# Roots by GpSimd's power and weight remainders by an accumulating DMA, in a two-layer diffusion trunk

## The chip, the cores and the metric

The kernel runs on one core of one Trainium2 chip. The metric is the device time of one execution in microseconds. Three timed runs of the kernel before took 2482.03, 2484.36 and 2476.64 us, so the median is 2482.03 us.

The engines are called PE (TensorE; PEld is its weight load), DVE (VectorE), ACT (ScalarE), POOL (GpSimd) and SP (SyncE, which here issues every DMA).

## The reference, cut to what matters

Two token streams of width 1024 (512 latent tokens and 128 context tokens) pass through two layers with the same weights. All arithmetic is float32.

```python
def rmsnorm(x, g):
    xf = x.astype(jnp.float32)
    y = xf * lax.rsqrt(jnp.mean(xf * xf, axis=-1, keepdims=True) + EPS)
    return (y * g.astype(jnp.float32)).astype(x.dtype)

def merge_branches(out_a, out_b, out_c, gates, lp, lam_init):
    oa = rmsnorm(out_a.reshape(B, L, A_HEADS, A_V), lp['a_subln_g']) * (1.0 - lam_init)
    ya = oa.reshape(B, L, A_WIDTH) @ lp['w_br_a']
    ...
    ga, gb, gc = jnp.split(jax.nn.sigmoid(gates), N_BRANCH, axis=-1)
    return (ga * ya + gb * yb + gc * yc) @ lp['w_out']

def latent_mixers(h, lp, lam, lam_init, cache, cos, sin):
    qa, ka, va, qb, kb, vb, qc, kc, vc, gates = project_heads(h, lp['w_in'])
    qb = apply_rope(rmsnorm(qb, lp['b_qnorm_g']), cos, sin)
    kb = apply_rope(rmsnorm(kb, lp['b_knorm_g']), cos, sin)
    ...

def trunk_layer(x, cvec, lp, mix_fn):
    sh1, sc1, g1, sh2, sc2, g2 = modulation(cvec, lp['w_mod'], lp['b_mod'])
    mixed, kv = mix_fn(rmsnorm(x, lp['norm1_g']) * (1.0 + sc1) + sh1)
    x = x + g1 * mixed
    x = x + g2 * swiglu(rmsnorm(x, lp['norm2_g']) * (1.0 + sc2) + sh2, lp['w_ffn_in'], lp['w_ffn_out'])
```

The norms that the change touches are those of `qb` (8 heads of 64), of `kb` (2 heads of 64) and of branch A's output (4 heads of 128). Each needs a reciprocal square root of a few numbers per token.

## The kernel before, in words

Each float32 product runs as three products in the faster type fp32r. A weight chunk of 128x1024 is loaded into `raw`. ACT copies it to `whi` (rounded to fp32r), POOL computes the remainder `wlo = raw - whi`, and PE multiplies `whi` with the high and low halves of the data and `wlo` with the high half (lines 410 to 412 for products with 320 columns, 718 to 720 for those with 256). There are 268 chunks. The buffers hold two `raw`, four `whi` and four `wlo`; `raw` is given back to the loader when `wlo` is done.

In each layer the first 60 chunks carry the q, k, v projections, the gates and the branch projections. They are used while the three attentions run, in the order of `STEPS`: the PE works on "dense" products wherever an attention item isn't ready. After them come the output projection (chunks from `O_WO` on), the second norm and the two parts of the FFN.

The order of every engine's instructions is fixed when the program is built. `_Order.run` is a list scheduler: tasks are Python generators that yield an engine, an estimated cost and a priority, and the scheduler picks the earliest by its estimates (`dve` is 0.068 us + 0.00104 us per element, `ptt` on POOL is 0.147 + 0.0021 per element). On the chip each engine runs its own list in that order and waits on semaphores, so an engine that stands at one instruction holds back all that is behind it.

The names that the change touches are these. `weights` has three tasks: `load` (SP's DMA into `raw`), `hi` (ACT's copy into `whi`) and `lo` (POOL's remainder into `wlo`). `rsqrt` computes 1/sqrt of a 128xn tile, with n of 2 (k norm), 4 (q norm) or 5 (branch A), on DVE alone: two integer instructions make a first guess in `rs_y`, and three Newton steps of three instructions each follow, with `rs_u` as scratch. `qk_norm` calls it 15 times in a layer and `a_head` four times, 38 calls in all. `rope` and `qk_norm` also use POOL for sums and products that feed the transposes of q and k (tiles `nat` and `st`).

Of the kernel before, what the change touches and what calls it, by code (L numbers as in the profile page):

```python
# [23 lines left out]

F32 = mybir.dt.float32
F32R = mybir.dt.float32r
I32 = mybir.dt.int32
AF = mybir.ActivationFunctionType
ALU = mybir.AluOpType
AX = mybir.AxisListType  # L30
# [2 lines left out]
P = 128  # L33
# [12 lines left out]
EPS = 1e-6  # L46
THETA = 10000.0
CH = 1024
MAGIC = 0x5F3759DF

C_ID, C_C, C_FG, C_END = 0, 128, 144, 152
S_N1, S_N2, S_BM, S_SUB, S_END = 0, 8, 16, 64, 65
# [6 lines left out]
O_WO = O_BR + 3 * N_BR  # L59
# [21 lines left out]


MOD_SOON, MOD_SPREAD = 0.7, 1.4
ENGINES = ("PE", "ACT", "DVE", "POOL", "SP")


# [4 lines left out]
class _Event:  # L91
    def __init__(self):
        self.t = None
        self.tasks = []
# [11 lines left out]
class _Order:  # L106


    def __init__(self):
        self.free = {e: 1.5 if e == "SP" else 2.9 for e in ENGINES}  # L110
        self.pend = {e: [] for e in ENGINES}
        self.slots = {}
# [75 lines left out]
    def run(self):  # L188
        while True:
            best = None  # L190
            for e in ENGINES:
                lst = self.pend[e]
# [31 lines left out]
def _n(ap):  # L224
    n = 1
    for d in ap.shape[1:]:
        n *= d
    return n
# [27 lines left out]
class _Trunk:  # L256
# [95 lines left out]
    def dma(self, out, in_, bytes_):  # L352
        return ("SP", max(0.45, bytes_ / 3.5e5), lambda: self.nc.sync.dma_start(out=out, in_=in_), 2.2)

    def weights(self, plan):

        self.chunks = []
        todo = []  # L360
        for p in plan:
            c = {"src": p, "loaded": self.ev(), "hi_ok": self.ev(), "lo_ok": self.ev()}
            todo.append(c)
        self.chunks = list(todo)

        def load(c):
            c["raw"] = yield from self.get("raw", [P, CH])
            yield self.dma(c["raw"], self.I["w"][c["src"]], 128 * 4 * CH)
            self.o.fire(c["loaded"])

        def hi():
            for c in todo:
                yield self.wait(c["loaded"])
                yield ("acq", "whi")
                yield ("acq", "wlo")
                c["hi"], c["lo"] = self.t("whi", [P, CH], F32R), self.t("wlo", [P, CH], F32R)
                yield self.act(c["hi"], c["raw"], AF.Copy)
                self.o.fire(c["hi_ok"])

        def lo():  # L380
            for c in todo:
                yield self.wait(c["hi_ok"])
                yield self.ptt(c["lo"], c["raw"], c["hi"].bitcast(F32), ALU.subtract)
                self.rel("raw")
                self.o.fire(c["lo_ok"])

        def load_rest():
            yield self.wait(todo[1]["loaded"])
            for c in todo[2:]:
                yield from load(c)  # L390

        for g in (load_rest, hi, lo):
            self.o.spawn(g(), 20)
        return [lambda c=c: load(c) for c in todo[:2]]
# [22 lines left out]

    def rsqrt(self, v, shape):

        nc = self.nc  # L420
        y = yield from self.get("rs_y", shape)
        u = yield from self.get("rs_u", shape)
        n = _n(v)
        yield self.dve(n, lambda: nc.vector.tensor_scalar(
            u.bitcast(I32), v.bitcast(I32), 1, None, op0=ALU.logical_shift_right))
        yield self.dve(n, lambda: nc.vector.tensor_scalar(
            y.bitcast(I32), u.bitcast(I32), -1, MAGIC, op0=ALU.mult, op1=ALU.add))
        for _ in range(3):
            yield self.tt(u, y, y, ALU.mult)
            yield self.stt(u, u, -0.5, v, ALU.mult, ALU.mult)  # L430
            yield self.stt(y, u, 1.5, y, ALU.add, ALU.mult)
        self.rel("rs_u")
        return y

# [261 lines left out]
    def qkv_unit(self, evac, n_slots, events):  # L696
# [51 lines left out]
        def run_by_rows():  # L748
# [13 lines left out]
            for b in (NB - 1, *range(NB - 1)):  # L762
                self.o.spawn(after(b, *ds[b]), 30 + 0.1 * b - (NB - 1 - b == 0))

        return run, run_by_rows

    def rope(self, x, b, groups, k=None):
# [788 lines left out]
    def layer(self, l, h, norm1, close):  # L1556
# [53 lines left out]
        def dense():  # L1610
            steps = _steps()
            if l == 0:
                yield from unit(*steps.pop(0))[1]()
            else:
                two = [unit(*steps.pop(0))[0] for _ in range(2)]
                for blocks in (range(2), range(2, NB)):
                    for run in two:
                        yield from run(blocks)
            for kind, i in steps:
                yield from step(kind, i)  # L1620
            yield self.wait(x2_open)
            halves = [(m, e) for m in range(WO_SPLIT) for e in range(2)]
            halves += [(m, e) for e in range(2) for m in range(WO_SPLIT, KT)]
            yield from self.out_proj(l, halves, x2, ssq2, ssq2_ok)
            o.fire(out_done)
            yield self.wait(f_open)
            for part in PARTS:
                yield from self.ffn_in(part, h2[0], h2[1], act, act_ok)
                if part[-1] == NF - 1:
                    yield self.wait(ssq3_open)  # L1630
                yield from self.ffn_out(l, part, act, act_ok, x2, ssq3, ssq3_ok, not last)
            o.fire(ffn_done)
# [144 lines left out]
    def run(self):  # L1777
        nc, I = self.nc, self.I
# [11 lines left out]
        pool, _ = self.bufs["c"]  # L1790
        one = lambda tag, shape: pool.tile(shape, F32, tag=tag, name=tag, bufs=1)
        con = one("con", [P, C_END])
        self.ident = con[:, C_ID:C_ID + P]
        self.fg = con[:, C_FG:C_FG + 8]
        self.ones, self.eps = one("ones", [P, P]), one("eps", [P, 1])
        cact = one("cact", [P, 16])
        self.cact = cact.rearrange("p (k c) -> p k c", k=KT)
        self.small, self.modc, self.acol, self.g1h, self.mod_ok = [], [], [], [], []
# [6 lines left out]
        nc.sync.dma_start(out=con, in_=I["con"])  # L1805
        nc.vector.memset(self.ones, 1.0)
        nc.vector.memset(self.eps, EPS)
        nc.scalar.activation(cact, con[:, C_C:C_C + 16], AF.Silu)
        for l in range(DEPTH):
            nc.sync.dma_start(out=self.small[l], in_=I["sm"][l])  # L1810
# [180 lines left out]
```

## Time and profile before

| | |
|---|---|
| median of three runs | 2482.03 us (2476.64 to 2484.36) |
| the profiled execution | 2480.7 us |
| its span, first to last instruction | 2478.9 us |
| mean granted TensorE clock | 0.983 of full speed |
| busy: PE, DVE, ACT, POOL | 96%, 66%, 44%, 37% |
| attention stages (PE interleaves attention and dense work) | about 62 to 640 us and 1302 to 1860 us of the span |

The profile comes from one execution on the chip. A line such as "L338 DVE ... x57 | 20.9, 373 | 0.4" tells source line, engine, output and input tiles, the count, busy microseconds and the mean nanoseconds of one, and then the idle time of the engine just ahead of these instructions with what ended it. The attention and FFN stages have different limits, so shares over the whole span say little about either.

### The profile page before, as it was taken

What the parts mean: (1) busy time and instruction counts of PE and PEld (TensorE: products, weight loads), DVE (VectorE), ACT (ScalarE), POOL (GpSimd) and SP (SyncE); (2) the same over time, 40 slices, a digit from 0 to 9 for tenths busy, and PEclk for the clock granted to TensorE, in tenths of its full rate; (3) what the DMA queues carried; (4) which work ended last, traced back from release to release, by engine and by line L of the source; (5) the groups of instructions that cost most, each with busy time, mean ns of one, the idle gap of its engine ahead of it and who ended that gap; (6) DMA issues with size and microseconds to landing.
All of it is one profiled execution on the core that took longest, in us unless ns stands there. A gap on an engine that the chain in (4) does not pass through costs nothing.

```text
span 2478.9 us, 44317 instructions
## 1 busy us (share of the span) xinstructions
PE 2381.0 (96%) x17084; PEld 2332.7 (94%) x17084; DVE 1646.1 (66%) x3924; ACT 1097.4 (44%) x2566; POOL 907.2 (37%) x656
## 2 busy tenths in 40 slices
PE   7998889999999999999989998999999999999997
PEld 4998889999988999999989997999999999999997
DVE  7588898678799666676677879887774462212224
ACT  5666566556323322122257664666552342212221
POOL 3534322433433433333345434224333343333331
PEclk9999999999999999999999999999999999999999
DMA  6211111111454444344422111101112322222221
GB/s 235 88 45 57 38 43 35 48 52 44 145 191 141 153 143 150 133 156 139 150 88 70 53 59 43 35 29 63 44 52 73 106 77 77 77 77 71 75 77 60
DMA packets 84739, 216.54 MB, mean 87 GB/s; under 512 B 9648, under 2 KB 23600, under 8 KB 84272
## 3 DMA queue, kind: packets, MB, share of 16 engines
q1 hardware_dynamic: 84528, 213.71, 25.6%
q8 instruction: 135, 2.21, 0.4%
q14 instruction: 76, 0.62, 0.1%
HBM read 206.85 MB, written 6.82 MB: 86 GB/s over the span
## 4 chain that ended last, share of the span: by engine, by line
PE 76%; DVE 18%; issue 2%; ACT 1%; DMA 1%; POOL 0%; SPq 0%; DVEq 0%; ACTq 0%
PE S L411 12%; PE S L410 12%; PE S L412 12%; PE B L410 6%; PE B L412 6%; PE B L411 6%; PE B L1024 3%; PE B L718 3%; PE B L720 3%; PE B L719 3%; PE S L996 2%; PE S L995 2%; DVE nu L338 2%; DVE P L346 2%; PE B L1260 2%
## 5 line engine op out<-in xcount | busy, mean ns | idle before, releaser
L350 POOL TENSOR_TENSOR wlo<-raw,whi 128x1024 fp32r<-128x1024 f32 x268 | 659.6, 2465 | 906.6 <-ACT whi L311 906.2
L411 PE MATMUL S<-h,whi 128*128 128x320 f32 x1408 | 438.7, 312 | 6.5 <-DVE h L338 5.8
L410 PE MATMUL S<-h,whi 128*128 128x320 f32 x1408 | 438.5, 311 | 0.0
L412 PE MATMUL S<-h,wlo 128*128 128x320 f32 x1408 | 437.4, 311 | 0.0
L311 ACT ACTIVATE whi<-raw 128x1024 fp32r<-128x1024 f32 x268 | 282.8, 1056 | 271.7 <-PE S L411 227.2
L718 PE MATMUL B<-whi,h 128*128 128x256 f32 x928 | 278.3, 300 | 1.0 <-DVE u L334 0.5
L411 PEld LDWEIGHTS S<-h,whi 128*128 128x128 f32 x1408 | 266.1, 189 | 9.4 <-DVE h L338 7.0
L720 PE MATMUL B<-whi,h 128*128 128x256 f32 x928 | 266.3, 287 | 3.7 <-DVE h L338 3.1
L410 PEld LDWEIGHTS S<-h,whi 128*128 128x128 f32 x1408 | 266.1, 189 | 0.8 <-ACT h L311 0.4
L412 PEld LDWEIGHTS S<-h,wlo 128*128 128x128 f32 x1408 | 266.3, 189 | 0.0
L719 PE MATMUL B<-wlo,h 128*128 128x256 f32 x928 | 265.7, 286 | 0.0
L515 DVE SCALAR_TENSOR_TENSOR md<-mr,cb 128x512 f32<-128x512 f32 x320 | 260.2, 813 | 5.5 <-DMA mr<-wt 0.8
L410 PE MATMUL B<-h,whi 128*128 128x320 f32 x768 | 245.2, 319 | 1.0 <-ACT th L311 1.0
L412 PE MATMUL B<-h,wlo 128*128 128x320 f32 x768 | 238.5, 311 | 0.0
L411 PE MATMUL B<-h,whi 128*128 128x320 f32 x768 | 238.2, 310 | 0.0
L334 DVE TENSOR_TENSOR s<-s,S 128x320 f32<-128x320 f32 x88 | 42.9, 488 | 281.2 <-ACT s L311 281.2
L311 ACT ACTIVATE P<-S,mx 128x768 f32<-128x768 f32 (+4 forms) x240 | 180.6, 754 | 88.3 <-DVE mx L1009 68.8
L410 PE MATMUL S<-act,whi 128*128 128x320 f32 x704 | 218.2, 310 | 0.0
L411 PE MATMUL S<-act,whi 128*128 128x320 f32 x704 | 217.8, 309 | 0.0
L412 PE MATMUL S<-act,wlo 128*128 128x320 f32 x704 | 217.7, 309 | 0.0
L410 PE MATMUL B<-u,whi 128*128 128x320 f32 x640 | 203.3, 318 | 5.2 <-ACT u L311 4.0
L411 PE MATMUL B<-u,whi 128*128 128x320 f32 x640 | 199.4, 312 | 0.8 <-DVE u L334 0.7
(162 smaller groups left out, 5918.3 us busy)
## 6 DMA issues: line engine op xcount, KB each, us to landing
raw<-w SPq DMA_DIRECT2D x268, 512.0 KB, 3.3
mr<-wt SPq DMA_DIRECT2D x160, 256.0 KB, 3.0
mraw<-wm SPq DMA_DIRECT2D x24, 256.0 KB, 4.8
x<-x SPq DMA_DIRECT2D x8, 320.0 KB, 5.6
xr<-x SPq DMA_DIRECT2D x16, 160.0 KB, 3.2
xm<-x SPq DMA_DIRECT2D x8, 320.0 KB, 4.3
xr<-xm SPq DMA_DIRECT2D x16, 160.0 KB, 2.6
y<-h SPq DMA_DIRECT2D x16, 160.0 KB, 1.8
```

Source lines behind the costliest of these rows:

```text
L311: fn = lambda: self.nc.scalar.activation(out, in_, func, **kw)
L338: _n(out), lambda: self.nc.vector.scalar_tensor_tensor(out, a, s, b, op0=op0, op1=op1),
L346: _n(out), lambda: self.nc.vector.tensor_scalar(out, a, s1, s2, op0=op0, **kw), not _in_psum(a), cols
L350: return ("POOL", 0.147 + 0.0021 * _n(out), lambda: self.nc.gpsimd.tensor_tensor(out, a, b, op=op), 0.08)
L410: mm(out, lhsT=wh, rhs=xh, start=first, stop=False)
L411: mm(out, lhsT=wh, rhs=xl, start=False, stop=False)
L412: mm(out, lhsT=wl, rhs=xh, start=False, stop=last)
L515: yield ("DVE", each, lambda w=d["raw"], b=b, r=r: nc.vector.scalar_tensor_tensor(md, w, 1.0, b, op0=ALU.mult, op1=ALU.mult, accum_out=r), ...
L718: mm(d, lhsT=hh, rhs=wh, start=kt == 0, stop=False)
L719: mm(d, lhsT=hh, rhs=wl, start=False, stop=False)
L720: mm(d, lhsT=hl, rhs=wh, start=False, stop=kt == KT - 1)
L1024: nc.tensor.transpose(t[:, i * P:(i + 1) * P], a, self.ident)
```

## The change

`rsqrt` keeps one Newton step of three DVE instructions. The first value is no longer made from two integer instructions on DVE; POOL computes v to the power of -0.5 against a tile `mhalf` that holds -0.5, set once at the start. The other two Newton steps are gone.

For the chunks from number 10 of the plan on that lie ahead of `O_WO` (110 of the 268: 50 in the first layer and all 60 in the second), ACT writes a second copy, `wlo = -raw` rounded to fp32r, and a DMA issued on POOL's queue adds `raw` to it in place. POOL's subtraction of 128x1024 is gone for these chunks. `raw` goes back to the loader when that DMA has landed. The scheduler is told 1.0 us of POOL and 4.5 us until landing for it.

```diff
+ADD_FROM = 10
...
+    def dma_add(self, out, in_):
+
+        return ("POOL", 1.0, lambda: self.nc.gpsimd.dma_start(out=out, in_=in_, accum_op=ALU.add), 4.5)
+
...
-        for p in plan:
-            c = {"src": p, "loaded": self.ev(), "hi_ok": self.ev(), "lo_ok": self.ev()}
+        for n, p in enumerate(plan):
+            c = {"src": p, "add": n >= ADD_FROM and p[1] < O_WO, "loaded": self.ev(), "hi_ok": self.ev(), "lo_ok": self.ev()}
...
                 yield self.act(c["hi"], c["raw"], AF.Copy)
+                if c["add"]:
+                    yield self.act(c["lo"], c["raw"], AF.Copy, scale=-1.0)
                 self.o.fire(c["hi_ok"])
...
-                yield self.ptt(c["lo"], c["raw"], c["hi"].bitcast(F32), ALU.subtract)
+                if c["add"]:
+                    yield self.dma_add(c["lo"].bitcast(F32), c["raw"])
+                else:
+                    yield self.ptt(c["lo"], c["raw"], c["hi"].bitcast(F32), ALU.subtract)
                 self.rel("raw")
...
-        yield self.dve(n, lambda: nc.vector.tensor_scalar(
-            u.bitcast(I32), v.bitcast(I32), 1, None, op0=ALU.logical_shift_right))
-        yield self.dve(n, lambda: nc.vector.tensor_scalar(
-            y.bitcast(I32), u.bitcast(I32), -1, MAGIC, op0=ALU.mult, op1=ALU.add))
-        for _ in range(3):
-            yield self.tt(u, y, y, ALU.mult)
-            yield self.stt(u, u, -0.5, v, ALU.mult, ALU.mult)
-            yield self.stt(y, u, 1.5, y, ALU.add, ALU.mult)
+        yield self.ptt(y, v, self.mhalf[:, 0:n], ALU.pow)
+        yield self.tt(u, y, y, ALU.mult)
+        yield self.stt(u, u, -0.5, v, ALU.mult, ALU.mult)
+        yield self.stt(y, u, 1.5, y, ALU.add, ALU.mult)
```

The scheduler then lays out all engines anew. In the whole program DVE's list goes from 3308 to 2994 rows, ACT's from 2088 to 2198, POOL's from 661 to 699; PE's and SP's keep their rows in a partly different order.

The first place is DVE at the first k norm of branch B in the first layer (tile `ss` holds the mean squares, `nat` the keys being normed; `P`, `PT` and `mx` belong to attention items, `acc` to their sums). Before, the list reads:

```order
L346 TENSOR_SCALAR ss_2245<-ss_2245 128x2
L1009 TENSOR_REDUCE mx_2248<-S_2220 128x1
L424 TENSOR_SCALAR rs_u_2280<-ss_2245 128x2
L426 TENSOR_SCALAR rs_y_2279<-rs_u_2280 128x2
L334 TENSOR_TENSOR rs_u_2280<-rs_y_2279 128x2
L338 SCALAR_TENSOR_TENSOR rs_u_2280<-rs_u_2280,ss_2245 128x2
L1119 RECIPROCAL acc_426_2137<-acc_426_2137 128x2
L338 SCALAR_TENSOR_TENSOR rs_y_2279<-rs_u_2280,rs_y_2279 128x2
L975 TENSOR_REDUCE ss_2296<-rp_459_2283 128x2
L334 TENSOR_TENSOR rs_u_2280<-rs_y_2279 128x2
```

And after the change, at the same norm:

```order
L346 TENSOR_SCALAR ss_2116<-ss_2116 128x2
L334 TENSOR_TENSOR rs_u_2128<-rs_y_2127 128x2
L338 SCALAR_TENSOR_TENSOR rs_u_2128<-rs_u_2128,ss_2116 128x2
L334 TENSOR_TENSOR u_1696<-B_2110,u_1696 128x128
L334 TENSOR_TENSOR u_1697<-B_2110,u_1697 128x128
L338 SCALAR_TENSOR_TENSOR rs_y_2127<-rs_u_2128,rs_y_2127 128x2
L338 SCALAR_TENSOR_TENSOR u_1695<-B_2118,u_1695 64x128 x2
L334 TENSOR_TENSOR nat_2102<-nat_2102,rs_y_2127 128x128
```

The two integer instructions and two of the three steps are gone; the row behind `ss` reads an `rs_y` that POOL writes, so DVE stands there until POOL has.

The second place is POOL around the same norm. Before, its list reads:

```order
L350 TENSOR_TENSOR st_2034<-rp_406_2035,rp_407_2036 128x256
L350 TENSOR_TENSOR wlo_2146<-raw_1773,whi_2145 128x1024
L350 TENSOR_TENSOR wlo_2170<-raw_1827,whi_2169 128x1024
L350 TENSOR_TENSOR kac_2288<-nat_2289,kac_2288 128x256
L350 TENSOR_TENSOR nat_2216<-nat_2216,sm_124 128x128
L350 TENSOR_TENSOR nat_2271<-nat_2271,sm_124 128x128
```

And after the change:

```order
L350 TENSOR_TENSOR st_1978<-rp_393_1979,rp_394_1980 128x256
L357 DMA wlo_2032<-raw_1758 128x1024
L350 TENSOR_TENSOR rs_y_2127<-ss_2116,mhalf 128x2
L357 DMA wlo_2056<-raw_1855 128x1024
L350 TENSOR_TENSOR nat_2102<-nat_2102,sm_126 128x128
L350 TENSOR_TENSOR st_2180<-rp_432_2181,rp_433_2182 128x256
```

The subtractions have become DMA issues at the same places, and the power of each root stands between them.

## Rows read from the trace of the kernel before

**Rows 1.** Page, busy time of the engines and the chain that ended last.

```profile
PE 2381.0 (96%) x17084; PEld 2332.7 (94%) x17084; DVE 1646.1 (66%) x3924; ACT 1097.4 (44%) x2566; POOL 907.2 (37%) x656
...
PE 76%; DVE 18%; issue 2%; ACT 1%; DMA 1%; POOL 0%; SPq 0%; DVEq 0%; ACTq 0%
```

**Rows 2.** Windows: length, busy per engine (instructions), granted clock, DMA share, GB/s.

```profile
124.00:434.00 310.00, 284.33 (x2190) 277.07 (x2189) 274.43 (x721) 191.08 (x511) 104.57 (x103) 0.97 0.13 43
434.00:640.00 206.00, 204.88 (x1576) 202.93 (x1575) 148.75 (x421) 123.45 (x325) 83.47 (x78) 1.00 0.15 52
682.00:806.00 124.00, 112.27 (x704) 108.03 (x703) 118.15 (x264) 41.68 (x76) 40.32 (x19) 0.93 0.49 166
1364.00:1674.00 310.00, 288.22 (x2239) 280.75 (x2238) 267.95 (x737) 190.81 (x516) 103.53 (x106) 0.98 0.13 44
1674.00:1860.00 186.00, 185.05 (x1409) 183.30 (x1408) 133.84 (x372) 109.09 (x280) 75.16 (x66) 1.00 0.16 53
```

**Rows 3.** Windows, single slices of 62 us, the same columns.

```profile
248.00:310.00 62.00, 55.51 (x431) 53.92 (x429) 55.31 (x193) 33.03 (x92) 21.16 (x19) 0.97 0.11 37
372.00:434.00 62.00, 59.47 (x468) 58.77 (x467) 54.81 (x109) 43.13 (x104) 14.59 (x14) 1.00 0.10 35
806.00:868.00 62.00, 62.00 (x425) 62.00 (x424) 41.47 (x86) 22.07 (x38) 24.81 (x11) 1.00 0.45 154
1488.00:1550.00 62.00, 50.28 (x353) 46.84 (x353) 60.65 (x209) 30.78 (x79) 26.14 (x24) 0.94 0.12 43
1550.00:1612.00 62.00, 60.48 (x463) 59.69 (x462) 53.78 (x110) 42.60 (x102) 13.93 (x13) 0.98 0.11 35
```

**Rows 4.** Windows of tile rs_u alone: length, DVE busy, clock, DMA share, GB/s.

```profile
248.00:310.00 62.00, 21.96 (x97) 0.97 0.11 37
372.00:434.00 62.00, 0.00 (x0) 1.00 0.10 35
1488.00:1550.00 62.00, 25.34 (x106) 0.94 0.12 43
```

**Rows 5.** Groups by line of DVE, 124 to 434 us.

```profile
L346 DVE TENSOR_SCALAR P<-P,acc 128x768 f32<-128x768 f32 (+1 forms) x34 | 27.8, 825 | 0.6
L338 DVE SCALAR_TENSOR_TENSOR rs_y<-rs_u,rs_y 128x4 f32<-128x4 f32 (+2 forms) x57 | 20.9, 373 | 0.4
...
L338 DVE SCALAR_TENSOR_TENSOR rs_u<-rs_u,ss 128x4 f32<-128x4 f32 (+2 forms) x57 | 11.9, 214 | 0.4
L334 DVE TENSOR_TENSOR rs_u<-rs_y 128x4 f32<-128x4 f32 (+2 forms) x57 | 11.4, 206 | 0.4
...
L426 DVE TENSOR_SCALAR rs_y<-rs_u 128x4 int32<-128x4 int32 (+2 forms) x19 | 7.8, 413 | 0.2
...
L424 DVE TENSOR_SCALAR rs_u<-ss 128x4 int32<-128x4 int32 (+2 forms) x19 | 5.0, 265 | 0.1
```

**Rows 6.** Timeline, 215 to 219 us: start, length, engine, line, tiles.

```profile
216.05 2.99 POOL L350 TENSOR_TENSOR wlo<-raw,whi 128x1024 fp32r<-128x1024 f32 x1
...
216.71 2.35 DVE L338 SCALAR_TENSOR_TENSOR rs_y<-rs_u,rs_y 128x2 f32<-128x2 f32 x1
```

**Rows 7.** Tiles rs_y and P on DVE, 124 to 434 us: count, ns min/median/max.

```profile
L338 DVE SCALAR_TENSOR_TENSOR rs_y<-rs_u,rs_y x57: 142/161/2370, 138.7 to 331.9; 128x4 f32<-128x4 f32 x30, 128x2 f32<-128x2 f32 x15, 128x5 f32<-128x5 f32 x12
...
L346 DVE TENSOR_SCALAR P<-P,acc x34: 279/620/2760, 313.8 to 430.3; 128x768 f32<-128x768 f32 x30, 128x128 f32<-128x128 f32 x4
```

**Rows 8.** Groups by line of POOL, 124 to 434 us.

```profile
L350 POOL TENSOR_TENSOR wlo<-raw,whi 128x1024 fp32r<-128x1024 f32 x22 | 53.7, 2445 | 44.7 <-ACT whi L311 44.7
...
L350 POOL TENSOR_TENSOR st<-rp,rp 128x256 f32<-128x256 f32 x12 | 9.6, 803 | 2.8 <-DVE rs_y L426 1.2 <-DVE rs_u L338 0.8 <-DVE ss L346 0.5
L350 POOL TENSOR_TENSOR nat<-rp,rp 128x128 f32<-128x128 f32 (+1 forms) x16 | 9.6, 598 | 37.6 <-DVE rp L334 12.6 <-DVE rs_u L334 6.2 <-DVE rs_u L338 5.8
```

**Rows 9.** Groups by line of ACT, 124 to 434 us.

```profile
L311 ACT ACTIVATE whi<-raw 128x1024 fp32r<-128x1024 f32 x22 | 23.2, 1056 | 3.8 <-PE B L411 2.1 <-issue 0.9 <-PE B L720 0.7
```

**Rows 10.** Waits of PE, 124 to 434 us: us in total, times, longest.

```profile
PE B L812 <- POOL nat L350: 6.3, 4, 4.7
...
PE S L995 <- ACT P L311: 1.1, 1, 1.1
```

**Rows 11.** Waits of PE, 1364 to 1674 us, the same columns.

```profile
PE S L995 <- ACT P L311: 2.9, 2, 1.8
```

**Rows 12.** Page, DMA issues: size and median us from issue to landing.

```profile
raw<-w SPq DMA_DIRECT2D x268, 512.0 KB, 3.3
```

More of the change, by code (lines that the diff above doesn't have):

```diff
@@ L26 @@
 F32R = mybir.dt.float32r
-I32 = mybir.dt.int32
 AF = mybir.ActivationFunctionType
@@ L48 @@
 CH = 1024
-MAGIC = 0x5F3759DF
 C_ID, C_C, C_FG, C_END = 0, 128, 144, 152
@@ L418, in rsqrt @@
     def rsqrt(self, v, shape):
-        nc = self.nc
         y = yield from self.get("rs_y", shape)
@@ L1794, in run @@
         self.fg = con[:, C_FG:C_FG + 8]
-        self.ones, self.eps = one("ones", [P, P]), one("eps", [P, 1])
+        self.ones, self.eps, self.mhalf = one("ones", [P, P]), one("eps", [P, 1]), one("mhalf", [P, 8])
         cact = one("cact", [P, 16])
@@ L1807, in run @@
         nc.vector.memset(self.eps, EPS)
+        nc.vector.memset(self.mhalf, -0.5)
         nc.scalar.activation(cact, con[:, C_C:C_C + 16], AF.Silu)
```

## The prediction

> **What bounds the kernel now.** I read the page first. PE is busy 96% of the span and the chain that ended last is PE for 76%, DVE for 18% [rows 1]. The reader is to see that nothing but PE's lost time can be won: 2478.9 - 2381.0 = 97.9 us of idle, plus what a lowered clock takes. Next the windows, to find where this lies. In the two stretches where the attention items are densest (124 to 434 us and 1364 to 1674 us) PE is idle 310 - 284.3 = 25.7 us and 310 - 288.2 = 21.8 us, at granted clocks of 0.97 and 0.98, while DVE is busy 274 and 268 of 310 us [rows 2]. In the attention's later part (434 to 640, 1674 to 1860) PE loses 1 us each, so what those stretches save on DVE buys nothing. Around the second norm of the first layer (682 to 806) PE idles 11.7 us, but there DVE works on the modulation, which the change leaves alone. In the FFN PE issues 425 matmuls in 62.0 us of 62.0 [rows 3]: no gain there either.
>
> So the ceiling is in the two stretches: 25.7 + 21.8 = 47.5 us of idle and, as the clock mean of 0.97 and 0.98 says, at most 310 x 0.03 + 310 x 0.02 = 15.5 us of slow clock, 63 us in all.
>
> Then slices inside the stretches. Where the roots stand thickest (tile rs_u takes 22.0 us of DVE in 248 to 310 and 25.3 us in 1488 to 1550 [rows 4]) PE loses 6.5 and 11.7 us; where there is no root (372 to 434, 1550 to 1612) it loses 2.5 and 1.5 us although DVE is still busy 54.8 and 53.8 of 62 [rows 3]. The idle time goes with the roots more than with DVE's load.
>
> **The roots.** In the first stretch there are 19 calls of eleven instructions: 20.9 + 11.9 + 11.4 + 7.8 + 5.0 = 57.0 us [rows 5]. At the median of 0.161 us [rows 7] they would be 19 x 11 x 0.161 = 33.6 us, so 23.4 us are stalls. The timeline shows one: POOL's remainder of a weight chunk runs from 216.05 for 2.99 us, and an instruction on 128x2 numbers that starts at 216.71 takes 2.35 us, until POOL is done [rows 6]. Three of eleven instructions stay (19 x 3 x 0.161 = 9.2 us), so DVE is rid of 19 x 8 x 0.161 = 24.5 us of work, and of most of the stalls by the next part.
>
> POOL's power is new. From below the nearest row is a sum of 128x128 or a little more at 0.60 us [rows 8], with fewer numbers here but more arithmetic in each; from above the whole remainder, 2.45 us. I take 0.6 us. DVE now stands between the mean squares and the first product until POOL has come to the power and done it; behind it in the list wait the rest of the step, the rope's copies and the attention's sums [the order in the section on the change]. Both hand-offs and what POOL has queued ahead cost DVE about 1 us a root in place of 1.3 us of instructions. That isn't all lost, since DVE idled 36 us of the first stretch anyway. For PE I set 6 us over the two stretches: about the 6.3 us that it now waits for POOL's nat tiles in one of them [rows 10].
>
> **The weights' remainder.** Between 124 and 434 us POOL spends 22 x 2.445 = 53.7 of its 104.6 busy us on it [rows 2, 8]. This goes, and with it the longest holders of what DVE waits for. Besides the 23.4 us of root stalls, the scaling of P takes 825 ns in the mean and 620 in the median, 34 x 0.205 = 7 us [rows 5, 7]. Of these 30 us I take two thirds, 20 us, as going, since the remainder is half of POOL's time and its longest instruction. DVE's first stretch falls to about 274 - 24.5 - 20 = 230 of 310 us, 74% in place of 89%.
>
> [...] No run here shows an issue from POOL yet.
>
> What it adds: ACT gets a copy of 1.056 us per chunk [rows 9], 22 x 1.056 = 23 us on 191 of the first stretch (62% to 69%), 46 us over both. It delays exponentials and transposes' copies. PE waits directly for ACT's P for 1.1 and 2.9 us [rows 10, 11]; I double this, + 4 us. The DMA issue on POOL is not in the trace: from below 0, from above as long as the subtraction (2.45 us) or longer, which is a rival. I take it below the subtraction. The landing takes at least what a load of the same 512 KB takes, 3.3 us [rows 12], and with a second read and a write on the same side perhaps twice, 6.6 us; I take 5. The two raw buffers then turn in 3.3 + 2 x 1.06 + 1 + 5 = 11.4 us, a chunk every 5.7 us. The greediest place, a gate, uses one chunk in 48 matmuls x 62.0 / 425 = 7.0 us [rows 3], and four chunks are kept ahead. So it stays hidden, up to a landing of 2 x 7.0 - 6.4 = 7.6 us in the worst place. SP's loads wait for the landing in place of the subtraction, and the caches' loads behind them too, with the same cover. DMA engines are 13% busy there [rows 2].
>
> **Sum.** I let the ten slices of the stretches come down to the two without roots: idle (2.5 + 1.5) / 2 = 2.0 us and clock (1.00 + 0.98) / 2, that is 0.6 us, a slice. Idle falls from 47.5 to 20, clock loss from 15.5 to 6: 37 us won. Less 6 for hand-offs and 4 for ACT: 27 us. From the profiled execution's 2480.7 us this gives 2453.7; the median of the runs is 1.3 us above it, so 2455 us. With costs between 0 and 20 us and the gain between 25 and 45 the case's own range is 2437 to 2477.
>
> **Rivals.**
> - *Everything in the stretches goes* because DVE at 74% never makes PE wait: 2480.7 - 63 + 1.3 = 2419 us. For it: DVE's load is the only one near full. Against: the slices without roots still lose time.
> - *The gain is eaten by other waits.* PE's waits are short and many, the longest for POOL's nat 4.7 us [rows 10], and the order is a new one, made with estimates; ACT at 69%, in order, puts copies of 1.06 us ahead of what PE needs. If of ACT's 46 us not 4 but half to three quarters, 23 to 34 us, pass to PE, the sum is 2455 + 19 = 2474 to 2455 + 30 = 2485; I take 2480, no change. For it: ACT is already 43 of 62 us in 372 to 434 [rows 3].
> - *The power doesn't relieve DVE.* If it takes as long as the remainder (2.45 us) plus its queue, DVE stands about 3 us a root, which is 57.0 / 19, what it spends now. [...]
> - *Slower: POOL's queue is held by the issues.* If writing out a 128-row DMA holds POOL for T, then at T = 5 us POOL is busy 50.9 + 22 x 5 = 161 of 310 us. A power or rope sum meets an issue 35% of the time and waits 2.5 us, 0.9 us in the mean in place of 17% x 1.2 = 0.2 us now. PE's waits for POOL's tiles (6.3 us) grow by four to 26, + 20 us a stretch: 2455 + 40 = 2495 us. It decides from about 4.3 us on, where it takes the 27 us back. Against it: nothing in the trace, which has no DMA from POOL.
>
> [...] I leave the rival's chance at 15%, no higher for it.
>
> **Chances.** The forecast 50%, all of it gone 8%, the power no relief 7%, the gain eaten 20%, POOL held 15%. A change within 0.3% (7.4 us: 2474.6 to 2489.5) can't be told from none. The eaten gain I split into 4, 14 and 2 for faster, same and slower, the held queue into 1 for the same and 14 for slower. Faster is 50 + 8 + 7 + 4 = 0.69, same 0.15, slower 0.16. The range 2428 to 2494 leaves out most of the second case below and half of the last above.
>
> **What would show it.** Right: DVE in the two stretches near 230 us; no DVE instruction on 128x4 of 2 us; PE idle some 10 us a stretch; spans of 1860 to 2479 us unchanged in length. Wrong: PE waiting for POOL's nat or st tiles in total over 15 us a stretch (held queue), PE or ACT waiting for DMA into wlo (late landing), PE waiting for ACT's P or PT over 10 us (ACT), gaps on DVE ahead of the roots' first product of over 2 us each (power).

## The result and the profile after

The changed kernel takes 2443.18 us, the median of four runs (2440.94 to 2450.73); beside it the kernel before took 2482.82 us (2476.64 to 2484.36). The ratio is 0.9854 (95% interval 0.9837 to 0.9871): faster, by about 40 us where 27 were forecast.

The first rows of the page after, busy time of the engines and the chain that ended last, answer to [rows 1]:

```profile
PE 2365.4 (97%) x17084; PEld 2322.6 (95%) x17084; DVE 1510.9 (62%) x3621; ACT 1195.5 (49%) x2676; POOL 773.6 (32%) x694
...
PE 77%; DVE 8%; issue 3%; DMA 2%; ACT 2%; POOL 1%; DVEq 0%; SPq 0%; POOLq 0%; ACTq 0%
```

DVE's share of the chain falls from 18% to 8%. The span is 2442.5 us, so PE idles 77.1 us in place of 97.9 ("idle" here is the span less PE's busy time). Its 17084 matmuls take 15.6 us less although they are the same: that is the granted clock, 0.990 over the span in place of 0.983. The profiled executions differ by 36.4 us = 20.8 of idle + 15.6 of clock.

Where it came from is read in the windows (length, busy per engine with the number of instructions, granted clock, DMA share, GB/s). After, to be held against [rows 2]:

```profile
124.00:434.00 310.00, 297.32 (x2365) 291.58 (x2364) 243.09 (x619) 225.06 (x577) 95.68 (x133) 1.00 0.34 85
434.00:640.00 206.00, 205.63 (x1557) 204.52 (x1556) 138.88 (x411) 134.66 (x313) 50.97 (x69) 1.00 0.45 113
682.00:806.00 124.00, 111.72 (x715) 108.24 (x714) 105.69 (x234) 47.29 (x86) 40.20 (x22) 0.96 0.49 163
1240.00:1302.00 62.00, 52.53 (x397) 50.78 (x395) 35.64 (x90) 44.18 (x107) 26.05 (x38) 0.94 0.56 138
1364.00:1674.00 310.00, 301.65 (x2383) 296.39 (x2382) 239.40 (x624) 224.35 (x566) 96.99 (x132) 1.00 0.37 91
1674.00:1860.00 186.00, 185.63 (x1377) 184.50 (x1376) 114.76 (x328) 115.48 (x264) 40.79 (x55) 1.00 0.42 104
```

And the one of these windows of the kernel before that stands in no group yet:

```profile
1240.00:1302.00 62.00, 55.50 (x392) 53.68 (x391) 43.78 (x95) 32.20 (x79) 30.17 (x31) 0.92 0.27 88
```

The two stretches lose 12.7 and 8.4 us where they lost 25.7 and 21.8, and both now run at a granted clock of 1.00. PE issues 2365 matmuls in the first 310 us in place of 2190. Around 1240 to 1302 us 3 us are lost that weren't before. So 47.5 - 21.0 = 26.5 us of idle are won in the stretches and 5.7 lost elsewhere.

PE's waits after (total, times, longest), 124 to 434 us, to be held against [rows 10]:

```profile
PE B L816 <- POOL nat L350: 1.8, 2, 1.1
PE B L1088 <- DVE onat L334: 1.8, 1, 1.8
PE B L1028 <- DVE P L346: 1.7, 1, 1.7
```

And over the whole span, two rows that the kernel before can't have:

```profile
PE B L723 <- DMA wlo<-raw: 5.0, 2, 4.7
...
PE B L421 <- DMA wlo<-raw: 2.7, 2, 2.0
```

PE waits 1.8 us for POOL's nat where it waited 6.3. The 5.0 us fall in 1240 to 1302, where the second layer's first chunks come up and 3 us more are lost than before; the 2.7 us fall in 640 to 682, where PE idles 2.0 us and before idled none.

The parts themselves. Groups by line of DVE after, 124 to 434 us (busy, mean ns, idle ahead of them), against [rows 5]:

```profile
L346 DVE TENSOR_SCALAR P<-P,acc 128x768 f32<-128x768 f32 (+1 forms) x40 | 22.1, 561 | 0.8
...
L334 DVE TENSOR_TENSOR rs_u<-rs_y 128x4 f32<-128x4 f32 (+2 forms) x19 | 7.1, 371 | 11.5 <-POOL rs_y L350 11.5
...
L338 DVE SCALAR_TENSOR_TENSOR rs_u<-rs_u,ss 128x4 f32<-128x4 f32 (+2 forms) x19 | 4.9, 264 | 0.2
...
L338 DVE SCALAR_TENSOR_TENSOR rs_y<-rs_u,rs_y 128x4 f32<-128x4 f32 (+2 forms) x19 | 3.1, 169 | 0.1
```

Tile rs_y over the same stretch (ns min/median/max), against [rows 7]:

```profile
L350 POOL TENSOR_TENSOR rs_y<-ss,mhalf x19: 709/1018/1468, 141.1 to 298.8; 128x4 f32<-128x4 f32 x10, 128x2 f32<-128x2 f32 x5, 128x5 f32<-128x5 f32 x4
L334 DVE TENSOR_TENSOR rs_u<-rs_y x19: 149/167/705, 142.5 to 299.9; 128x4 f32<-128x4 f32 x10, 128x2 f32<-128x2 f32 x5, 128x5 f32<-128x5 f32 x4
L338 DVE SCALAR_TENSOR_TENSOR rs_y<-rs_u,rs_y x19: 146/155/379, 144.2 to 302.7; 128x4 f32<-128x4 f32 x10, 128x2 f32<-128x2 f32 x5, 128x5 f32<-128x5 f32 x4
```

And the remainder: tile wlo over the span, then the page's DMA issues (size, median us from issue to landing):

```profile
L350 POOL TENSOR_TENSOR wlo<-raw,whi x158: 2387/2415/2977, 30.8 to 2400.6; 128x1024 fp32r<-128x1024 f32 x158
L311 ACT ACTIVATE wlo<-raw x110: 1040/1050/1082, 108.5 to 1877.1; 128x1024 fp32r<-128x1024 f32 x110
L357 POOL DMA_DIRECT2D wlo<-raw x110: 859/890/1077, 109.9 to 1878.5; - x110
```

```profile
wlo<-raw POOLq DMA_DIRECT2D x110, 512.0 KB, 4.8
```

The roots take 7.1 + 4.9 + 3.1 = 15.1 us of DVE where they took 57.0. In the rows of tile rs_y the longest root instruction is 0.71 us, where it was 2.37; over the whole span the longest is one of 1.43 us, which stands beside two of POOL's sums in a row. The power takes 1.02 us, an issue 0.89, the landing 4.8, and DVE stands 11.5 us at the power.

### The profile page after: what moved, and what is told of

It reads as the page before. It is cut to its first block, busy times and chain, and to the rows that moved or that the text cites. A ratio compares the mean times of both kernels' runs of the same rounds, so it can differ in the third digit from the quotient of the medians.

```text
span 2442.5 us, 44315 instructions
## 1 busy us (share of the span) xinstructions
PE 2365.4 (97%) x17084; PEld 2322.6 (95%) x17084; DVE 1510.9 (62%) x3621; ACT 1195.5 (49%) x2676; POOL 773.6 (32%) x694
## 4 chain that ended last, share of the span: by engine, by line
PE 77%; DVE 8%; issue 3%; DMA 2%; ACT 2%; POOL 1%; DVEq 0%; SPq 0%; POOLq 0%; ACTq 0%
PE S L420 13%; PE S L419 13%; PE S L421 13%; PE B L419 6%; PE B L421 6%; PE B L420 6%; PE B L1028 4%; PE B L722 2%; PE B L723 2%; PE B L724 2%; PE S L1000 2%; PE S L999 2%; PE B L1264 2%; PE B L1263 2%; DVE md L519 1%
## 5 line engine op out<-in xcount | busy, mean ns | idle before, releaser
L350 POOL TENSOR_TENSOR wlo<-raw,whi 128x1024 fp32r<-128x1024 f32 x158 | 390.2, 2471 | 694.1 <-ACT whi L311 693.8
L722 PE MATMUL B<-whi,h 128*128 128x256 f32 x928 | 274.3, 296 | 1.5 <-ACT nat L311 1.5
L724 PE MATMUL B<-whi,h 128*128 128x256 f32 x928 | 263.4, 284 | 2.2 <-POOL h L350 2.2
L519 DVE SCALAR_TENSOR_TENSOR md<-mr,cb 128x512 f32<-128x512 f32 x320 | 247.0, 772 | 20.8 <-DMA mr<-wt 16.0
L419 PE MATMUL B<-u,whi 128*128 128x320 f32 x640 | 202.5, 316 | 5.3 <-ACT u L311 4.2
L311 ACT ACTIVATE s<-S 128x320 f32<-128x320 f32 x88 | 38.5, 438 | 333.1 <-PE S L421 333.1
```

The costliest lines, as they stand in the source:

```text
L311: fn = lambda: self.nc.scalar.activation(out, in_, func, **kw)
L350: return ("POOL", 0.147 + 0.0021 * _n(out), lambda: self.nc.gpsimd.tensor_tensor(out, a, b, op=op), 0.08)
L419: mm(out, lhsT=wh, rhs=xh, start=first, stop=False)
L519: yield ("DVE", each, lambda w=d["raw"], b=b, r=r: nc.vector.scalar_tensor_tensor(md, w, 1.0, b, op0=ALU.mult, op1=ALU.mult, accum_out=r), ...
L722: mm(d, lhsT=hh, rhs=wh, start=kt == 0, stop=False)
L724: mm(d, lhsT=hl, rhs=wh, start=False, stop=kt == KT - 1)
```

## The experiments

"Idle" comes from the profiled execution. The kernel before, run again beside each group of experiments, had medians of 2481.79 to 2484.95 us. The ratios are to those; a difference of medians from two groups can be off by some 3 us for it.

| run | median us | ratio to before (95%) | idle | clock |
|---|---|---|---|---|
| changed kernel | 2443.18 | 0.9854 (0.9837 to 0.9871) | 77.1 | 0.990 |
| e1 roots only | 2471.69 | 0.9958 (0.9944 to 0.9972) | 91.1 | 0.984 |
| e2 remainder only | 2456.23 | 0.9893 (0.9879 to 0.9906) | 82.2 | 0.985 |
| e3 short root on DVE | 2471.11 | 0.9953 (0.9940 to 0.9965) | 92.7 | 0.984 |
| e4 ACT's copy twice | 2486.81 | 1.0011 (1.0002 to 1.0020) | 105.2 | 0.981 |
| e6 no Newton step | 2457.96 | 0.9896 (0.9880 to 0.9913) | 80.2 | 0.984 |
| e10 order alone | 2526.08 | 1.0176 (1.0159 to 1.0194) | 123.5 | 0.974 |
| e11 zero by POOL | 2463.04 | 0.9921 (0.9906 to 0.9936) | 85.3 | 0.987 |
| e14 fewer chunks | 2445.28 | 0.9850 (0.9835 to 0.9865) | 76.2 | 0.989 |
| e15 changed, estimates as measured | 2452.06 | 0.9881 (0.9866 to 0.9897) | 78.3 | 0.985 |
| e5 changed, issue told as 2.3 us | 2471.19 | 0.9960 (0.9947 to 0.9973) | 93.6 | 0.985 |
| e17 no step, estimates as measured | 2446.72 | 0.9868 (0.9852 to 0.9883) | 71.0 | 0.986 |
| e16 before, POOL as measured | 2495.26 | 1.0055 (1.0042 to 1.0068) | 106.6 | 0.982 |

My theory was that DVE was relieved twice, of root instructions and of POOL's hold on it (2.35 us beside a subtraction of 2.99 [rows 6]; e1's expectation calls it the lock), and that PE's idle time fell with it. The rivals were that one half does all of it, that the new order does it, and that ACT's or POOL's new work is where more could be won.

### Each half alone: e1 and e2

The first leaves the weights' remainder as it was; the second keeps the roots as they were.

```diff
-ADD_FROM = 10
+ADD_FROM = 10 ** 9
```

> Only the roots change; POOL still subtracts for all 268 chunks. Theory A (DVE is relieved by two halves of like size, fewer root instructions and no long POOL subtraction beside them): about half the gain, 2482 - 18 = 2464 us, DVE in 124 to 434 us near 250 of 310 us, and some DVE instructions of two operands still last over 2 us. Rival B (only the lock matters; the root's instructions cost nothing by themselves): 2478 to 2484 us. Rival C (the new order of the lists brings the gain, not the cheaper work): any value, not tied to DVE's busy time.

> Only the weights' remainder changes (110 accumulating DMAs); the roots are the eleven DVE instructions of before. Theory A: about half the gain, 2462 to 2468 us; the root instructions fall to a mean of about 0.16 us each, since a DMA issue of 0.9 us on POOL doesn't hold DVE, so the 23 us of root stalls in a stretch go. If an issue holds DVE as the subtraction did, their mean stays above 0.2 us. Rival B: nearly the whole gain, 2443 to 2450 us.

e1 wins about 10 us, e2 about 26; the product of the ratios, 0.9958 x 0.9893 = 0.9851, is that of both together. So the halves aren't of like size, which the first theory took them to be: e1 comes out between the first theory's 2464 us and its rival's 2478 to 2484, and e2 between 2462 to 2468 and its rival's 2443 to 2450. The stretches in e1, then in e2 (columns as above):

```profile
124.00:434.00 310.00, 287.94 (x2251) 281.66 (x2251) 255.14 (x591) 197.81 (x532) 121.89 (x123) 0.98 0.14 44
...
1364.00:1674.00 310.00, 292.49 (x2295) 287.84 (x2294) 246.49 (x592) 196.12 (x527) 126.78 (x126) 0.98 0.14 44
```

```profile
124.00:434.00 310.00, 293.90 (x2317) 288.50 (x2315) 256.63 (x763) 223.01 (x573) 73.86 (x110) 0.98 0.34 82
...
1364.00:1674.00 310.00, 298.68 (x2346) 293.02 (x2345) 247.63 (x754) 221.72 (x565) 73.28 (x110) 0.98 0.36 86
```

DVE is equally busy in both, 255 and 257 us of the first stretch, yet the stretches' idle time is 39.6 us in e1 and 27.4 in e2. Summed over PE's waits in both stretches, those that DVE ends are 30.6 us before, 29.6 in e1, 13.5 in e2 and 10.7 after; those that POOL ends are 12.3, 3.9, 4.6 and 7.0. So e1 wins at POOL's tiles, which stand behind the roots, and PE's waits for DVE fall only when the subtraction is gone. Tile rs_y over the span in e1, then in e2:

```profile
L334 DVE TENSOR_TENSOR rs_u<-rs_y x38: 143/283/2368, 140.4 to 1528.1; 128x4 f32<-128x4 f32 x20, 128x2 f32<-128x2 f32 x10, 128x5 f32<-128x5 f32 x8
```

```profile
L336 DVE TENSOR_TENSOR rs_u<-rs_y x114: 133/155/731, 144.6 to 1516.9; 128x4 f32<-128x4 f32 x60, 128x2 f32<-128x2 f32 x30, 128x5 f32<-128x5 f32 x24
```

In e1 instructions on 128x4 numbers still take 2.37 us, and its timeline (start, length, engine, line, tiles) shows beside what:

```profile
140.35 2.40 POOL L350 TENSOR_TENSOR wlo<-raw,whi 128x1024 fp32r<-128x1024 f32 x1
140.44 2.34 DVE L334 TENSOR_TENSOR rs_u<-rs_y 128x5 f32<-128x5 f32 x1
...
143.13 2.34 POOL L350 TENSOR_TENSOR wlo<-raw,whi 128x1024 fp32r<-128x1024 f32 x1
143.23 2.27 DVE L338 SCALAR_TENSOR_TENSOR rs_y<-rs_u,rs_y 128x5 f32<-128x5 f32 x1
```

Both DVE instructions end with POOL's. In e2, with issues in the remainder's place, the longest of all its 418 root instructions is 0.73 us; in the first stretch they take 40.6 us, 0.19 each, where it was 57.0 before. Counted over the span, nine of e1's two-input root instructions (those of the Newton step) start while a subtraction runs and take 1.07 to 2.37 us (in the kernel before 16 do, of which 11 take 1.46 to 2.37 us and five 0.15; of the integer instructions, with one input, three do, of which two take 2.32 us and one 0.15); 46 of the changed kernel and e2 start while an issue runs, and 45 of them take 0.13 to 0.19 us, one 0.31. So the subtraction held DVE and the issue doesn't. The changed kernel's timeline shows both: a root instruction held by a smaller product of POOL, and a scaling beside an issue:

```profile
285.41 0.74 POOL L350 TENSOR_TENSOR nat<-nat,sm 128x256 f32<-128x256 f32 x1
285.50 0.67 DVE L338 SCALAR_TENSOR_TENSOR rs_u<-rs_u,ss 128x4 f32<-128x4 f32 x1
...
300.48 0.61 DVE L346 TENSOR_SCALAR P<-P,acc 128x768 f32<-128x768 f32 x1
300.49 0.92 POOL L357 DMA_DIRECT2D wlo<-raw  x1
```

The root instruction ends with POOL's product, 0.67 us for a median of 0.16. The scaling and the issue take what they take elsewhere: the scaling 0.61 us against a median of 0.62 [rows 7], the issue 0.92 against 0.89.

### The hand-off to POOL: e3

The kernel before with one Newton step in place of three, the first guess still made by DVE.

```diff
-        for _ in range(3):
+        for _ in range(1):
```

> The kernel before with one Newton step in place of three, the integer guess staying on DVE: the roots are less exact, nothing runs on POOL for them. Against e1 it tells the price of the hand-off to POOL and of its power. If the hand-off costs the 6 us that I set: 6 us below e1, near 2458. If POOL's power is as cheap as the two integer instructions: equal to e1 within 3 us. If the lists' order decides (C): no relation.

2471.11 us against e1's 2471.69: by this pair the power and its hand-off cost what the two integer instructions cost, as far as two different lists can tell (see the last group of runs). The groups by line fit it. The five instructions of e3's roots take 7.7 + 7.1 + 6.0 + 5.4 + 4.9 = 31.1 us between 124 and 434 us; the three of e1 take 12.5 + 7.6 + 5.6 = 25.7 us, and DVE stands 5.1 us at the power, 30.8 in all.

### The order alone: e10

The instructions of before, with the scheduler told that eight of a root's eleven take nothing and the remainder 1.0 us of POOL, as it is told of the changed kernel.

```diff
+                op = self.ptt(c["lo"], c["raw"], c["hi"].bitcast(F32), ALU.subtract)
+                yield (op[0], 1.0, op[2], 1.5) if c["src"][1] < O_WO else op
...
+        low = lambda op: (op[0], 0.001, op[2], 0.0)
```

> Rival C by itself: all instructions of the kernel before, but the scheduler is told that eight of a root's eleven instructions take nothing and that the subtraction ahead of the output projection takes 1.0 us of POOL, so the lists are laid out much as in the changed kernel. Theory A (cheaper work, not the order): no gain, 2478 to 2490 us. Rival C: most of the gain, under 2460 us.

Slower by 43 us, where 2478 to 2490 was expected for my theory. This isn't the changed kernel's order itself, which has instructions that this kernel lacks. But an order made for cheaper work, where the work isn't gone, brings nothing and costs much. PE's waits over its span:

```profile
PE B L815 <- POOL nat L350: 26.3, 13, 6.3
PE B L1087 <- DVE onat L334: 19.8, 7, 6.1
```

### ACT's price: e4 and e11

e4 writes the negative copy twice; e11 leaves it out, lets POOL set wlo to zero and adds raw to that, so that its wlo holds raw and not the remainder.

```diff
                 if c["add"]:
                     yield self.act(c["lo"], c["raw"], AF.Copy, scale=-1.0)
+                    yield self.act(c["lo"], c["raw"], AF.Copy, scale=-1.0)
```

```diff
-                if c["add"]:
-                    yield self.act(c["lo"], c["raw"], AF.Copy, scale=-1.0)
...
                 if c["add"]:
+                    yield ("POOL", 1.0, lambda: self.nc.gpsimd.memset(c["lo"].bitcast(F32), 0.0), 0.08)
```

> The changed kernel with ACT's copy of -raw made twice (110 more copies of 1.056 us, 116 us of ACT). Tells what ACT's added work costs. With my price of 4 us for 46 us of ACT in the two stretches: 2443 + 4 to 6 = 2448. If ACT is near to being the bound: 2443 + 20 or more. If it is free: 2443 within 2.

> ACT's copy of -raw is left out; POOL writes zeros into wlo in its place and the DMA adds raw, so the products are not the reference's. Tells what ACT's first 116 us cost, and whether a POOL instruction that only writes SBUF holds DVE. If ACT's first copies are hidden (theory A after the doubled copy cost 43 us: the cost rises steeply only past some load): 2440 to 2446 us. If they cost in proportion to the doubling: 2443 - 30 = 2413 us or less. If the write-only instruction holds DVE, the mean of the root instructions rises from 0.17 to over 0.25 us.

One more copy of 1.05 us for each of 110 chunks makes it 43.6 us slower than the changed kernel (39 by the ratios), all that was won, where my price of ACT gave 2448, with ACT at only 239 and 232 us of the stretches' 310. The four largest of PE's waits in e4, over the span:

```profile
PE B L817 <- POOL nat L350: 14.7, 5, 7.0
PE S L1000 <- ACT P L311: 6.8, 3, 4.6
PE B L619 <- DVE ssq L334: 6.8, 5, 2.7
PE B L866 <- POOL st L350: 6.7, 6, 4.4
```

Two of the four name POOL, though POOL has no more to do than in the changed kernel. An issue stands on POOL until ACT's copy is done, and POOL starts nothing else meanwhile: after, 22.6 us in seven waits, as POOL's own waits show (1364 to 1674 us):

```profile
POOL wlo L357 <- ACT wlo L311: 22.6, 7, 5.8
```

But that isn't what made the longest of e4's waits. Its timeline at the second longest for nat:

```profile
273.25 0.72 POOL L350 TENSOR_TENSOR nat<-rp,rp 128x256 f32<-128x256 f32 x1 [1.46 <-DVE rp L334]
273.95 0.94 POOL L357 DMA_DIRECT2D wlo<-raw  x1
274.03 0.47 PE L817 MATMUL B<-con,nat 128*128 128x128 f32 x1 [4.92 <-POOL nat L350]
```

The issue comes behind the sum that PE waits for, and POOL stood for DVE's rope products (rp). At the longest, 7.0 us, POOL's last wait is again for DVE, and the issue ahead of it started without waiting. So PE's wait names POOL where POOL had waited for DVE. How the copy's 43.6 us come about stays open.

e11 takes ACT's added copies out and is 20 us slower than the changed kernel all the same, over both of the times expected (2440 to 2446, or 2413 and less). POOL now has a memset per chunk, as the groups by line between 124 and 434 us show:

```profile
L388 POOL MEMSET wlo<- 128x1024 f32 x23 | 22.2, 964 | 38.0 <-PE B L420 38.0
```

So a memset of 0.96 us on POOL did no better here than the copy of 1.05 us on ACT. The price of ACT's first copy by itself stays open, since no run takes it away without adding elsewhere.

e11 tells more of POOL's hold on DVE. Its stretches, and a root instruction beside a memset:

```profile
124.00:434.00 310.00, 298.44 (x2351) 292.62 (x2351) 246.51 (x613) 204.69 (x552) 118.55 (x154) 0.99 0.34 83
...
1364.00:1674.00 310.00, 298.92 (x2362) 293.54 (x2362) 234.45 (x610) 199.46 (x542) 117.61 (x157) 0.99 0.37 90
```

```profile
140.75 0.94 POOL L388 MEMSET wlo<- 128x1024 f32 x1
140.82 0.16 DVE L334 TENSOR_TENSOR rs_u<-rs_y 128x5 f32<-128x5 f32 x1
```

The 15 root instructions that start while a memset runs take 0.15 to 0.17 us: a memset doesn't hold them. (The mean of all root instructions in the first stretch, 0.28 us, is over the 0.25 that was to tell of a hold; but it is 0.26 in the changed kernel, which has no memset there.) POOL is nearly as busy as in e1 (119 and 118 us for 122 and 127) and ACT too (205 and 199 us for 198 and 196), with the same short roots; yet the stretches' idle time is 22.6 us where e1 has 39.6. The lists differ as well, but this points to POOL's hold on DVE and not to how busy POOL is. The 20 us that e11 loses to the changed kernel lie elsewhere: only 1.6 us of them are idle time of the stretches.

### Less work, and no faster: e6, e14

e6 drops the Newton step, so that the power is the whole root. e14 uses the new path for chunks 10 to 51 of each layer only, which leaves the second layer's first chunks to POOL's subtraction.

```diff
-        yield self.tt(u, y, y, ALU.mult)
-        yield self.stt(u, u, -0.5, v, ALU.mult, ALU.mult)
-        yield self.stt(y, u, 1.5, y, ALU.add, ALU.mult)
```

```diff
-            c = {"src": p, "add": n >= ADD_FROM and p[1] < O_WO, "loaded": self.ev(), ...
+            c = {"src": p, "add": ADD_FROM <= n % N_CH < ADD_TO, "loaded": self.ev(), ...
```

> The Newton step behind POOL's power is left out, three more DVE instructions of 0.16 us a root (18 us over the kernel). If DVE still bounds the attention stretches: 2443 - 6 = 2437 us, in the proportion that e1 showed (13 us for 49 us of clean DVE work). If DVE no longer bounds them: 2443 within 3.

> The accumulating DMA only for the chunks 10 to 51 of each layer's 134; the first ten of the second layer and the last eight ahead of the output projection of both go back to POOL's subtraction. In the changed kernel PE waits 5.0 us for wlo at the start of the second layer and 2.7 us between 640 and 810 us, where the DMA engines are 85 to 90% busy. If these waits are the late landing: 2443 - 6 to 8 = 2436 us. If subtraction only puts other waits there: 2443 within 3.

Neither is faster. e6 is 15 us slower than the changed kernel, with three instructions less in each of 38 roots, which neither of its two expectations allowed; e14 is the same, as the second of its two had it. In e14 PE's waits for wlo are gone, and between 1240 and 1302 us PE is busy 55.80 us, as before the change (55.50), and not 52.53. But the 3.3 us don't reach the end: the second stretch now idles 10.9 us in place of 8.4, and PE's busy time over the span is 2.0 us longer at a clock of 0.989. In e6 the stretches (windows):

```profile
124.00:434.00 310.00, 298.50 (x2356) 292.54 (x2356) 235.35 (x561) 226.47 (x583) 94.70 (x130) 0.98 0.34 84
...
1364.00:1674.00 310.00, 295.86 (x2301) 290.48 (x2300) 225.32 (x543) 216.51 (x551) 92.23 (x126) 0.98 0.35 85
```

DVE has less to do, yet the clock is 0.98. Of the 15.8 us between the spans, 12.7 are PE's busy time at the lower clock and 3.1 idle. That pointed to the list and not to the work, which the last four runs tested.

### How far lists of the same work lie apart: e15, e5, e17, e16

Only numbers told to the scheduler differ: e15 is the changed kernel with the power told as 1.0 us and the issue as 0.89 + 3.9 us, e17 the same without the Newton step, e5 the changed kernel with the issue told as 2.3 us, e16 the kernel before with the remainder told as measured (2.45 us).

```diff
-        yield self.ptt(y, v, self.mhalf[:, 0:n], ALU.pow)
+        yield ("POOL", 1.0, lambda: self.nc.gpsimd.tensor_tensor(y, v, self.mhalf[:, 0:n], op=ALU.pow), 0.08)
...
-        return ("POOL", 1.0, lambda: self.nc.gpsimd.dma_start(out=out, in_=in_, accum_op=ALU.add), 4.5)
+        return ("POOL", 0.89, lambda: self.nc.gpsimd.dma_start(out=out, in_=in_, accum_op=ALU.add), 3.9)
```

> The changed kernel with the same instructions, only the scheduler's estimates put at what the trace after shows: the power 1.0 us in place of 0.147 + 0.0021 per element, the issue of the adding DMA 0.89 us and 3.9 us more until landing. Theory A (of the 36 us of gain the work removed gives the most, the list only a few us): 2435 to 2448 us. Theory B (the changed kernel's list is a lucky one, and any other list of the same work is 10 to 20 us slower): 2453 to 2463 us, with granted clocks of 0.97 to 0.98 in the stretches 124 to 434 and 1364 to 1674 us.

> The changed kernel with the same instructions, the scheduler told that the issue of the adding DMA takes 2.3 us of POOL in place of 1.0. It is told wrongly, so a list a little worse is expected: theory A (the work decides) 2443 to 2455 us, since POOL's list then is spread out like that of the kernel before. Theory B (lists of the same work lie 15 us and more apart) 2455 to 2470 us.

> Power alone, without the Newton step, as in the run that was 15 us slower than the changed kernel, but with the scheduler told 1.0 us for the power and 0.89 us for the issue. Theory A (that run's loss was its list, and the list was poor because a power told as 0.15 us takes 1.0): 2435 to 2445 us. Theory B (leaving out the step makes a new wait, whatever the list): 2453 to 2463 us.

> The kernel before with the same instructions, the scheduler told 0.00225 us per element of a POOL instruction in place of 0.0021, which makes the remainder 2.45 us as measured in place of 2.30. It measures how far lists of the same work lie apart for the kernel before. Theory A: within 8 us of before, 2475 to 2490 us. Theory B (the list counts as much as the change): more than 15 us from it on one side.

e15, e17 and e16 fall between their theories, e15 a microsecond short of the second; e5 lies above both. With truer estimates the changed kernel is 9 us slower, and the one before 13 us slower; a false one costs the changed kernel 28 us. Without the Newton step the new list is 11 us faster than e6's and within 4 us of the changed kernel: most of the loss was the list. Like with like, the change wins 39.6 us (2482.82 to 2443.18) and, with measured estimates on both sides, 2495.26 - 2452.06 = 43.2 us. All three lists of the changed work (2443, 2452 and 2471 us) lie below both of the old (2483 and 2495). So that there is a gain isn't a lucky list, but its size depends on the pair that is taken, from 12 us to 52, and any difference of 10 to 15 us between two kernels here may be a list. That holds for e1's 10 us against e2's 26 and their product, for e3 and e1, for e11's 20 in part, and for e14 and e17, which don't beat the changed kernel. The changed kernel's four runs alone reach from clocks of 0.991 (2440.94 us) to 0.988 (2450.73 us).

The stretches' idle time separates the runs better than the whole time does. In the five runs whose chunks are all subtracted on POOL it is 39.6 (e1), 41.7 (e3), 47.5 (before), 52.0 (e16) and 69.4 us (e10); in the eight with the accumulating DMA and no doubled copy it is 21.0 (after) to 27.4 us (e2). Only e4, with ACT's copy twice, has 43.4. The lists differ within either group; the groups don't overlap.

e5 shows how a told number turns into a wait. Its largest wait of PE over the span, which isn't among the changed kernel's largest:

```profile
PE B L816 <- ACT nat L311: 11.5, 4, 3.1
```

Half of it (5.8 us) falls in 434 to 640 us and half in 1674 to 1860, where the changed kernel loses 0.4 us each; e5 loses 6.5 us in either.

## Why the prediction was right

- **What bounds the kernel: right.** All the idle time that was won lies in the two stretches. I let their idle time fall from 47.5 to 20 us; it fell to 21.0. I let the clock give back 9.5 of 15.5 us there; with 1.00 in both windows it gave all of it, and over the span PE's busy time fell by 15.6. These 6 us are half of the 12 by which the forecast was too cautious.
- **The roots: right in size, and by two causes.** 57.0 us should become 9.2; they became 15.1. e1 shows why both halves are needed: with the remainder still on POOL, 57 instructions take 25.7 us, of which 16.5 are stalls by the same median of 0.161 us. What stays of stalls after, 15.1 - 9.2 = 5.9 us, stands beside POOL's smaller sums and products, as at 285.50: of the 31 root instructions of over 0.3 us in the whole span, 30 end with one. DVE as a whole fell to 243 and 239 us, not 230; the stretches hold 8% and 6% more matmuls (2365 for 2190, 2383 for 2239), and so more of the attention's own DVE work.
- **The power: duration mis-sized, price too high.** I took 0.6 us and it takes 1.02. DVE stands at it 11.5 / 19 = 0.6 us a root, within the 1 us that I allowed. But the 6 us charged to PE aren't seen: its wait for POOL's nat in the first stretch fell by 4.5 us, and e3 equals e1, within what two lists can tell.
- **POOL's hold on DVE: right.** I let 20 of 30 us of stalls go with the subtraction; that an issue wouldn't hold DVE as the subtraction does was an assumption, since no run before the change showed an issue from POOL. The runs bear it out: 2.34 us beside the subtraction (e1), 0.67 beside a product of 0.74, but 0.16 beside a memset (e11), and 0.13 to 0.19 beside an issue, for 45 of 46. Of the 110 issues none took over 1.08 us.
- **ACT: the price isn't shown, and the way that I gave for it isn't seen.** I doubled PE's direct waits for ACT in the stretches and got 4 us more; all such waits there fell, from 4.3 us to 2.6. Yet e4's second copy of the same size goes with 43.6 us, more than the 28 us of e5's false estimate, though no more than e10's, so a part of it may be the list. PE's longest waits in e4 name POOL, and POOL had waited for DVE. The rival in which the gain is eaten was nearer than my 20% had it, by one copy a chunk.
- **Transfers: right, with one place missed.** Landing 4.8 us for 5 taken. The row I named for a late landing, PE waiting for DMA into wlo, shows 7.7 us, of which 5.0 at the second layer's start, a place that I had not looked at. With the 3.0 and 2.0 us that PE idles more in those two places they are most of what the stretches' gain lost outside them (5.7 us); in e14, which has neither wait, that loss is 2.9 us.
- **Sum.** Of the forecast, 37 less 10; of the trace, 26.5 + 15.6 - 5.7 = 36.4 us. The step that failed is the 10 us: its two parts are not in the places where I put them, and 5.7 us stand elsewhere. And the clock's 9.5 us was 6 us too small. That the forecast of 2455 us came within 12 us is in part luck: with the same work and truer estimates the list gives 2452 (e15), with a false one 2471 (e5).
- **Signs.** No root instruction lasts 2 us, PE idles 12.7 and 8.4 us a stretch, and the last 4063 matmuls, those behind 1860 us before, take 619.8 us where they took 619.1: as I had said. DVE's 243 and 239 us are above the 230 that I named.
- **Rivals.** The held queue needed an issue of 4.3 us; it takes 0.89. The power was no remainder (1.02 us for 2.45). "Everything goes" was too much: 21.0 us of the stretches' idle stay, spread over many waits of under 2 us.

## What to carry to other kernels

When a small instruction on one engine lasts as long as a large one on another, price the large one's removal by the stalls that it causes, not by its own engine's busy share: e2 removed no instruction from DVE and won more than e1, which removed 304. DVE's own busy time doesn't tell the two apart; what ended PE's waits does. Follow the list of each engine that gets new work: the wait may carry another engine's name, as e4's waits for POOL do. And where a scheduler builds the lists, take the spread of lists with the same work (9 to 28 us here, 43 where they were made for other work) as the resolution, whatever the runs' own interval says.

## What the runs showed of the hardware that was not expected

- An accumulating DMA of 512 KB within SBUF lands in 4.8 us, where a load of as much takes 3.3 [rows 12], and its issue holds POOL for 0.89 us.
- Beside POOL's subtractions, sums and products of two tensors most of DVE's root instructions last until POOL's is done (2.34 us beside 2.40 in e1; in the kernel before 11 of the 16 two-input ones that start beside a subtraction, up to 2.37 us, and two of the three with one input, 2.32 us); beside an issue (0.13 to 0.19 us for 45 of 46 root instructions) and a memset (0.15 to 0.17 us for 15) they don't.
- POOL's power on 128x2 to 128x5 takes 1.02 us, more than its sum of 128x256 (0.80 us [rows 8]).
- A memset of 128x1024 on POOL takes 0.96 us (e11), 40% of the subtraction of that size (2.42 us).
- The granted clock isn't told by a window's idle time alone: after the change PE idles 9.1 us between 248 and 310 us at 1.00, where before it idled 6.5 us at 0.97 [rows 3]. After, that slice reads:

```profile
248.00:310.00 62.00, 52.89 (x413) 50.44 (x413) 50.87 (x155) 41.38 (x108) 31.61 (x37) 1.00 0.32 84
```
